# Places of TensorE's operands, dummy products ahead of runs of 256-column products, one more pair of feed-forward blocks by seven products, and half a conditioning vector made earlier

## The chip, the cores and the metric

The kernel runs on one core of a Trainium2 chip. The metric is the device time of one execution in microseconds (us), the median of the runs. TensorE is called PE in the profile, its weight loads PEld, VectorE DVE, ScalarE ACT, GpSimd POOL and SyncE SP.

## What is computed

Two layers over 512 tokens of width 1024, in float32. Layer 0 mixes tokens with a gated linear recurrence (hgrn2), layer 1 with attention in three dilated groups; each is followed by a gated feed-forward network (FFN) of inner width 2816.

```python
cond = silu(c)
h = x
for layer in range(2):
    mod = (cond @ ada_w[layer] + ada_b[layer])[:, None, :]
    sh1, sc1, g1, sh2, sc2, g2 = split(mod, 6)
    u = rms_norm(h, norm_g[layer, 0]) * (1 + sc1) + sh1
    y = hgrn2_mixer(u, ...) if layer == 0 else dilated_attention_mixer(u, ...)
    h = h + (1 + g1) * rms_norm(y, norm_g[layer, 1])
    u = rms_norm(h, norm_g[layer, 2]) * (1 + sc2) + sh2
    gate, up = split(u @ ffn_w_in[layer], 2)
    y = (silu(gate) * up) @ ffn_w_out[layer]
    h = h + (1 + g2) * rms_norm(y, norm_g[layer, 3])
```

The six vectors of `mod` are the conditioning vectors; the text writes (layer, number, half) for a half of 512, so (1, 1, 0) is the first half of layer 1's `sc1`.

## The kernel before

**Products of float32 values.** Every large operand is cut into two parts, a high part `hi` (rounded to the matmul's float32r type by ACT) and a low part `lo = x - hi` (DVE). One product of blocks is three matmuls: hi by hi, hi by lo, lo by hi. The activations stand in `uh` and `ul`, in the attention also, with the tokens in another order, in `apart` (two tiles). A matmul streams its moving operand, 512 or 256 columns, past a stationary operand (the weights that PEld loads, 128 columns). A row of the profile names them `out<-moving,stationary`. Products with 256 moving columns are called narrow here.

**FFN, first half.** `PLAIN = (3, 2)` says how many pairs of 256 columns of gate and up are made plainly in layer 0 and in layer 1: per pair 4 blocks of 24 matmuls with 512 columns (`block`, lines 577 to 579). The first pair is made in the stage before (`mixer_out`), by halves of the tokens. The other blocks of 128 columns, 22 - 2 * `PLAIN`, are made by `seven_products`: gate and up times the two halves of the tokens are a 2 by 2 product of blocks, done with seven block products instead of eight. Each of the seven is 12 narrow matmuls (`run`, line 964), so a block is 84. The sums of activations they need, `th` and `tl`, come from `token_sums` after the first plain pair; the sums of weights are made by POOL and DVE while PE works on the block before. The places of the cut weights (`ring`, `spare`) begin `R0 = 16` columns, 64 bytes, behind a multiple of 128 bytes; `uh`, `ul`, `th`, `tl` begin at multiples of 128 bytes. One of the seven products, `first`, uses the quarter B11 of the activations. For the first block it takes it where it stands; then `shift` copies this quarter 144 columns on (576 bytes, so 64 behind a multiple of 128), and every later block reads it there:

```python
B11 = [u_of(0, 0), [(uh[:, k, 144:400], ul[:, k, 144:400]) for k in range(4)]]
...
run(s.first, R, 0, B11[i > 0], True)
run(s.both, Sm, 1024, T3, True)
```

**Attention.** Queries and keys of two of the three groups are made by seven products as well (`sevens`, narrow, weights at `R0`, moving operands at multiples of 128 bytes), those of the third plainly with 512 columns. The values of two groups are made by `value_unit`, four times seven products of two by 12 narrow matmuls. There the activations are the stationary operand (multiples of 128 bytes) and the cut weights move; their places begin at `V0 = 32` columns, 128 bytes. All this is ordered by a planner (`Plan`): tasks with costs and due times are placed in a simulated run of the engines, and the order found is then issued as it is. `products` (line 1976) adds one task of 6 or 12 matmuls.

**Loads.** All weights come through one list, `items`, by SP's queue into a ring of two places `raw` of 1 MB; a load starts when the item two places earlier has been used. Items of the conditioning weights are woven between the others by `weave(list, others, first, every)`: one group of `others` after each `every` items of the list. Most conditioning halves are summed over k by DVE, four operations for each 1 MB item, and over the partitions by POOL (`partition_all_reduce`); for those in `sum_by_pe` the second sum is four PE products with `ones` (line 421), and for those in `by_pe` PE does both (line 372).

Of the kernel before, what the change touches and what calls it, by code (L numbers as in the profile page):

```python
# [11 lines left out]
F32 = mybir.dt.float32  # L12
# [5 lines left out]
P = 128  # L18
# [15 lines left out]
MAGIC = 12582912.0  # L34
WHOLE = ("quarters", "half")

R0, V0 = 16, 32


class Stream:  # L40
# [100 lines left out]
class Plan:  # L141
# [3 lines left out]
    DRAIN = {"DVE": 0.12, "ACT": 0.12}  # L145

    def __init__(self):
        self.tasks, self.names, self.seq = [], {}, {}

    def add(self, eng, cost, fn=None, r=(), w=(), goal=None, late=None, urgent=False):  # L150

# [85 lines left out]
    def run(self):  # L237

        ts = self.tasks
        for t in ts:  # L240
            for d in t["deps"]:
                ts[d]["outs"].append(t["id"])
        due = [0.0] * len(ts)
        for t in reversed(ts):
            at = min([due[o] - self.after(t, ts[o]) for o in t["outs"]], default=1e9)
            if t["goal"] is not None:
                at = min(at, t["goal"] + t["cost"])
            due[t["id"]] = at - t["cost"]
        tries = (self.trial(due, *rule) for rule in itertools.product((1, 2, 3, 5), (0.1, 0.2, 0.3), (5.0, 8.0, 1e9), (0.3, 1.0)))
        end, done, start = min(tries, key=lambda r: r[0])  # L250
        for t in done:
            t["start"], t["due"] = start[t["id"]], due[t["id"]]
        for t in done:
            if t["fn"]:
                t["fn"](t["eng"])
        return done
# [36 lines left out]
def block_kernel(tc, x, c, positions, ada_w, ada_b, norm_g, hgrn_w_in, lower, hgrn_norm_g, hgrn_w_out,  # L293
# [8 lines left out]
    with ExitStack() as ctx:  # L302
# [55 lines left out]
            return shared[:, 2 + turns_of_acc[0] % 2]  # L358

        by_pe = lambda l, v, hf: l == 0 and v in (2, 3, 4)  # L360
        sum_by_pe = lambda l, v, hf: by_pe(l, v, hf) or (l, v) == (1, 4)

        def ada_groups(l, v, hf, kq):

# [122 lines left out]
        items = []  # L487
# [6 lines left out]
        hg.append(win(W, 3 * D + 3 * 256))  # L494
        hg_o = [wtok(hgrn_w_out[0], kq, hf * 512) for hf in range(2) for kq in range(2)]

        PLAIN = (3, 2)

        def ffn_ws(l):

# [4 lines left out]
                a.append(("quarters", tuple(w[:, c:c + P].rearrange("(k p) n -> p k n", p=P) for c in (DFF + f * P, f * P))))  # L505
            return a, [wrow(ffn_w_out[l], j) for j in range(NF // 2)]

        items += weave(hg, ada_seq((0, 2), (0, 4), (0, 3), (1, 4)), 1, 0.7) + hg_o
        f0a, f0b = ffn_ws(0)
        n0 = 2 * PLAIN[0]  # L510
        gate, gate_fins = ada_halves(0, 5)
        one, two = ada_seq((1, 1)), ada_seq((1, 0))
        items += weave(f0a[:n0], [one[0], one[1], [], one[3][:1]], 2) + f0a[n0:]
        late = [gate[0], gate[1], gate[2], gate_fins[:1] + gate[3], one[2], gate_fins[1:] + one[3][1:], two[0], one[5] + two[1]]
        items += weave(f0b, late + two[2:], 0, 0.95)
        AW = attn_w_in[0]

        def av(g, hf):
# [363 lines left out]
        def seven_products(fs, mid, seeded, spare, th, tl):  # L882
# [5 lines left out]
            t_of = lambda i: [(th[:, i, k], tl[:, i, k]) for k in range(4)]  # L888
            B21, B22 = u_of(1, 0), u_of(1, 1)

            B11 = [u_of(0, 0), [(uh[:, k, 144:400], ul[:, k, 144:400]) for k in range(4)]]

            def shift():

                for a, b in ((112, 256), (0, 112)):
                    for copy, t in ((act.copy, uh), (dve.tensor_copy, ul)):
                        copy(t[:, 0:4, a + 144:b + 144], t[:, 0:4, a:b].bitcast(F32))
            t1, T3, T4, t2 = (t_of(i) for i in range(4))

            W = shared.rearrange("p a (b n) -> p (a b) n", b=2)  # L900
# [74 lines left out]
            with tc.manual_schedule(engines=ORDERED):  # L975
                r_hi(0)
                r_lo(0)
                sum_a(0)
                sum_b(0)
                sum_c(0)  # L980
                for k in range(2):
                    s_hi(0, k)
                    s_lo(0, k)
                r_hi(1)
                before = None
                for i in range(len(fs)):
                    more = i + 1 < len(fs)
                    R, Sm = places(i)
                    s = Sums(i)
                    run(s.first, R, 0, B11[i > 0], True)  # L990
                    run(s.both, Sm, 1024, T3, True)
                    if before:
                        gate_of(i - 1, before)
                    act.copy(s.u2, s.first)
                    if more:
                        r_lo(i + 1)
                        sum_a(i + 1)
                    if before:
                        value_of(i - 1, before)
                    run(s.u2, Sm, 0, t2, False)  # L1000
                    run(s.first, R, 1024, B21, False)
                    act.copy(W[:, 4 + i % 2], s.both)
                    act.copy(s.u4, s.u2)
                    if i == 0:
                        shift()
                    run(s.u4, Sm, 512, t1, False)
                    run(s.u2, R, 512, T4, False)
                    if more:
                        sum_b(i + 1)
                        s_hi(i + 1, 0)  # L1010
# [878 lines left out]
        def PE(cost, fn, r=(), w=()):  # L1889
            plan.add("PE", cost, lambda e: fn(), r, w, goal=clock[0])  # L1890
            clock[0] += cost
# [81 lines left out]
        def split_place(first):  # L1973
            return plan.place("hl", 3, lambda: st.part_tiles(first))

        def products(cost, dst, key, terms, begin, reads):


            def go():
                todo = [p for t in terms() for p in t]  # L1980
                for i, (x, y) in enumerate(todo):
                    pe.matmul(dst(), x, y, start=begin and i == 0, stop=i == len(todo) - 1, skip_group_check=True)  # L1982
            of_units.append(len(plan.tasks))
            PE(cost, go, reads, [key])

        triple = lambda xh, xl, yh, yl: ((xh, yh), (xh, yl), (xl, yh))
        a_of = lambda r, c: [[a[:, r * 4 + k, c * 256:c * 256 + 256] for a in apart] for k in range(4)]
# [117 lines left out]
        def plain(g, hd):  # L2105
# [16 lines left out]
            def both():  # L2122
# [4 lines left out]
                def one(i, t):  # L2127
                    b = mm_of()
                    for part in range(4):
                        def terms(part=part):  # L2130
                            for kt in (2 * part, 2 * part + 1):
                                w = slice((i * KT + kt) * P, (i * KT + kt + 1) * P)
                                yield triple(p.t[0][:, w], p.t[1][:, w], apart[0][:, kt], apart[1][:, kt])
                        products(6 * 0.2275, lambda: b.t, b(), terms, part == 0, [p("h", i), p("l", i)])
                    scale = SCALE if i == 0 else 1.0
                    for hf in range(2):
                        o = i * 64 + hf * 32
# [12 lines left out]
        def value_unit(i, hf):  # L2150
# [46 lines left out]
            def run(tag, tile, o, us):  # L2197
                b, p = mm_of(tag), ps[tile]
                for n in range(2):
                    def terms(n=n):  # L2200
                        for kt in range(4):
                            w = slice(o * 1024 + kt * 256, o * 1024 + (kt + 1) * 256)
                            yield triple(*us(kt, n), p.t[0][:, w], p.t[1][:, w])
                    products(12 * 0.1165, lambda n=n: b.t[:, n * 256:(n + 1) * 256], b(), terms, n == 0, [p("h", o), p("l", o)])
                return b

            def add_to(out, one, b, f):
# [293 lines left out]
```

## Time and profile before

| | |
|---|---|
| median of 3 runs | 1506.12 us (1504.59 to 1506.7) |
| profiled execution, its own time | 1504.35 us |
| its span | 1502.6 us |
| PE busy | 1476.8 us, 98% |
| PEld busy | 1323.5 us, 88% |
| DVE, ACT, POOL busy | 1095.8, 797.2, 191.3 us |
| bytes | 201.09 MB, mean 134 GB/s |

Matmuls overlap in the pipeline, so the length shown for one (276 to 281 ns for a narrow one) is not what it costs. What it costs is its pitch, the time from its start to the start of the next. A pitch is read here from a stretch that PE fills without a wait: its length over the number of matmuls that begin in it. In the view by windows the count of PE (x...) holds also the one or two that began just before the stretch.

The stages in the profiled execution: layer 0's mixer to about 300 us, the end of `mixer_out` to 341, layer 0's FFN to about 690, the attention to about 1110, layer 1's FFN after that, its narrow products from 1203.4 to 1376.5.

### The profile page before, as it was taken

Reading aid. Unit: us, or ns where it says so; the run is one execution under the profiler, and the core shown is the slowest. Engines: PE = TensorE matmul, PEld = TensorE weight load, DVE = VectorE, ACT = ScalarE, POOL = GpSimd, SP = SyncE. Lnnn points to the kernel's source line nnn. Section 1 sums busy time; section 2 is a strip of 40 time slices with the busy share of each in tenths; the row PEclk is TensorE's granted clock in tenths of the full one; section 3 lists DMA queues with packets and bytes.
Section 4 is the critical chain, followed back from the end, with each engine's and each line's share of the span. In section 5 each row is a group of like instructions: output and inputs, shape, how many; then the busy total and the mean of one; then the engine's idle time right before and its main releaser. Section 6 shows DMA issues by size and latency. Waiting matters only on the chain. (4 is left out here: it accounts for less than half of the span.)

```text
span 1502.6 us, 25061 instructions
## 1 busy us (share of the span) xinstructions
PE 1476.8 (98%) x9823; PEld 1323.5 (88%) x9823; DVE 1095.8 (73%) x1800; ACT 797.2 (53%) x1474; POOL 191.3 (13%) x172
## 2 busy tenths in 40 slices
PE   8999999999999999999999999999989999999998
PEld 6777788888999988788999999999978899999886
DVE  4587678487688885777798877888666978887533
ACT  4433343373455542267647878477875555555231
POOL 1011011031111100131001010001012211110100
PEclk9999999999999999999999999999999999999999
DMA  9654555124233346634344442345243333333531
GB/s 308 183 170 140 183 169 169 57 79 146 85 113 113 113 161 211 220 117 143 113 120 144 109 136 73 118 131 147 89 134 119 104 94 113 113 113 141 197 111 56
DMA packets 210151, 201.09 MB, mean 134 GB/s; under 512 B 8248, under 2 KB 167920, under 8 KB 209776
## 3 DMA queue, kind: packets, MB, share of 16 engines
q1 hardware_dynamic: 207056, 192.71, 41.3%
q10 hardware_dynamic: 1952, 6.65, 1.2%
q8 instruction: 77, 1.26, 0.4%
q0 software_dynamic: 1024, 0.13, 0.2%
q14 instruction: 42, 0.34, 0.1%
HBM read 192.31 MB, written 5.31 MB: 132 GB/s over the span
## 5 line engine op out<-in xcount | busy, mean ns | idle before, releaser
L90 ACT CAST hi<-raw 128x2048 fp32r<-128x2048 f32 x43 | 82.1, 1909 | 144.3 <-DMA raw<-in_ffn_w_out_dram 74.9
L91 DVE TENSOR_TENSOR lo<-raw,hi 128x2048 fp32r<-128x2048 f32 x43 | 103.7, 2413 | 65.7 <-ACT hi L90 65.6
L577 PE MATMUL ps_mm<-uh,hi 128*128 128x512 f32 (+1 forms) x400 | 145.6, 364 | 0.0
L578 PE MATMUL ps_mm<-ul,hi 128*128 128x512 f32 (+1 forms) x400 | 144.5, 361 | 1.1 <-DVE ul L677 1.1
L579 PE MATMUL ps_mm<-uh,lo 128*128 128x512 f32 (+1 forms) x400 | 143.9, 360 | 0.0
L1982 PE MATMUL ps_mm<-apart,hiq 128*128 128x256 f32 (+1 forms) x608 | 142.0, 326 | 0.1
L1982 PEld LDWEIGHTS ps_mm<-apart,hiq 128*128 128x128 f32 x608 | 100.0, 189 | 8.4 <-ACT xs L2096 0.3
L1982 PE MATMUL ps_mm<-apart,loq 128*128 128x256 f32 (+1 forms) x304 | 97.4, 321 | 0.4 <-DVE loq L2118 0.4
L964 PE MATMUL ps_mm<-tl,hiq 128*128 128x256 f32 x340 | 94.0, 276 | 0.0
L964 PE MATMUL ps_mm<-th,hiq 128*128 128x256 f32 x340 | 94.0, 276 | 0.0
L964 PE MATMUL ps_mm<-th,loq 128*128 128x256 f32 x340 | 94.0, 276 | 0.0
L955 DVE TENSOR_TENSOR loq<-raw,hiq 128x1024 fp32r<-128x1024 f32 x68 | 80.3, 1221 | 18.6 <-ACT hiq L951 18.6
L577 PEld LDWEIGHTS ps_mm<-uh,hi 128*128 128x128 f32 x400 | 75.2, 188 | 18.2 <-issue 6.7
L578 PEld LDWEIGHTS ps_mm<-ul,hi 128*128 128x128 f32 x400 | 75.4, 189 | 12.3 <-DVE ul L677 1.5
L579 PEld LDWEIGHTS ps_mm<-uh,lo 128*128 128x128 f32 x400 | 75.1, 188 | 12.4 <-issue 1.1
L578 PE MATMUL ps_mm<-lo,oh 128*128 128x512 f32 x208 | 81.5, 392 | 2.4 <-DVE lo L91 2.4
L935 POOL TENSOR_TENSOR raw<-raw 128x512 f32<-128x512 f32 x34 | 44.8, 1318 | 303.1 <-DVE spare L931 138.5
L577 PE MATMUL ps_mm<-hi,oh 128*128 128x512 f32 x208 | 81.5, 392 | 0.0
L951 ACT CAST hiq<-raw 128x1024 fp32r<-128x1024 f32 x68 | 68.0, 1047 | 18.7 <-DVE raw L939 17.1
L1982 PE MATMUL ps_mm<-uh,hiq 128*128 128x256 f32 x256 | 71.9, 281 | 0.0
L1982 PE MATMUL ps_mm<-uh,loq 128*128 128x256 f32 x256 | 71.3, 279 | 0.0
L1982 PE MATMUL ps_mm<-ul,hiq 128*128 128x256 f32 x256 | 71.3, 278 | 0.0
(479 smaller groups left out, 4632.8 us busy)
## 6 DMA issues: line engine op xcount, KB each, us to landing
raw<-in_ada_w_dram SPq DMA_DIRECT2D x40, 1024.0 KB, 5.1
raw<-in_ffn_w_in_dram SPq DMA_DIRECT2D x136, 256.0 KB, 4.1
raw<-in_ffn_w_out_dram SPq DMA_DIRECT2D x22, 1024.0 KB, 5.1
raw<-in_attn_w_in_dram SPq DMA_DIRECT2D x64, 256.0 KB, 4.6
raw<-in_hgrn_w_in_dram SPq DMA_DIRECT2D x12, 1024.0 KB, 5.3
raw<-in_attn_w_in_dram SPq DMA_DIRECT2D x12, 1024.0 KB, 5.2
raw<-in_ffn_w_in_dram SPq DMA_DIRECT2D x10, 1024.0 KB, 6.5
raw<-in_attn_w_in_dram SPq DMA_DIRECT2D x16, 512.0 KB, 4.6
```

What stands on the lines that cost most here:

```text
L90: self.nc.scalar.copy(hi, t)
L91: self.nc.vector.tensor_sub(lo, t, hi.bitcast(F32))
L577: pe.matmul(ps, ah, bh, start=start, stop=False, skip_group_check=part)
L578: pe.matmul(ps, ah, bl, start=False, stop=False, skip_group_check=part)
L579: pe.matmul(ps, al, bh, start=False, stop=stop, skip_group_check=part)
L935: pool.tensor_add(r[:, 2], r[:, 2], r[:, 0])
L951: act.copy(hi, src)
L955: dve.tensor_sub(lo, src, hi.bitcast(F32))
L964: pe.matmul(ps, w[x][:, a], us[kt][y], start=begin and kt + m == 0, stop=kt == 3 and m == 2, skip_group_check=True)
L1982: pe.matmul(dst(), x, y, start=begin and i == 0, stop=i == len(todo) - 1, skip_group_check=True)
```

## The change

```diff
-R0, V0 = 16, 32
+R0, V0 = 16, 48
...
+        narrow = []
+        for t in [t for t in done if t["eng"] == "PE"] + [{}]:
+            if t.get("narrow"):
+                narrow.append(t)
+                continue
+            first = next((k for k, u in enumerate(narrow) if u["aside"]), len(narrow))
+            if len(narrow) - first >= 12:
+                self.asides.add(narrow[first]["id"])
+            narrow = []
...
-        sum_by_pe = lambda l, v, hf: by_pe(l, v, hf) or (l, v) == (1, 4)
+        sum_by_pe = lambda l, v, hf: by_pe(l, v, hf) or (l, v) == (1, 4) or (l, v, hf) == (1, 1, 0)
...
-        PLAIN = (3, 2)
+        PLAIN = (2, 2)
...
-        items += weave(hg, ada_seq((0, 2), (0, 4), (0, 3), (1, 4)), 1, 0.7) + hg_o
+        one, two, own = ada_seq((1, 1)), ada_seq((1, 0)), ada_seq((0, 2), (0, 4), (0, 3), (1, 4))
+        items += weave(hg, own[:16] + [one[0], own[17] + one[1]], 1, 0.55) + hg_o[:1] + one[3][:1] + hg_o[1:]
...
-        n0 = 2 * PLAIN[0]
         gate, gate_fins = ada_halves(0, 5)
-        one, two = ada_seq((1, 1)), ada_seq((1, 0))
-        items += weave(f0a[:n0], [one[0], one[1], [], one[3][:1]], 2) + f0a[n0:]
         late = [...]
-        items += weave(f0b, late + two[2:], 0, 0.95)
+        items += f0a + weave(f0b, late + two[2:], 0, 0.95)
...
-            B11 = [u_of(0, 0), [(uh[:, k, 144:400], ul[:, k, 144:400]) for k in range(4)]]
-
-            def shift():
-
-                for a, b in ((112, 256), (0, 112)):
-                    for copy, t in ((act.copy, uh), (dve.tensor_copy, ul)):
-                        copy(t[:, 0:4, a + 144:b + 144], t[:, 0:4, a:b].bitcast(F32))
+            B11 = u_of(0, 0)
...
-                    run(s.first, R, 0, B11[i > 0], True)
+                    run(s.first, R, 0, B11, True)
+                    if i == 0:
+                        for _ in range(3):
+                            pe.matmul(s.both, R[0][:, 0:P], uh[:, 0, 16:272], start=True, stop=True, skip_group_check=True)
                     run(s.both, Sm, 1024, T3, True)
...
-                    if i == 0:
-                        shift()
...
+                for _ in range(3 if me in plan.asides else 0):
+                    pe.matmul(dst(), todo[0][0], aside(), start=True, stop=True, skip_group_check=True)
                 for i, (x, y) in enumerate(todo):
                     pe.matmul(dst(), x, y, start=begin and i == 0, stop=i == len(todo) - 1, skip_group_check=True)
...
-                    products(12 * 0.1165, lambda n=n: b.t[:, n * 256:(n + 1) * 256], b(), terms, n == 0, [p("h", o), p("l", o)])
+                    products(12 * 0.1165, lambda n=n: b.t[:, n * 256:(n + 1) * 256], b(), terms, n == 0, [p("h", o), p("l", o)],
+                             lambda: p.t[0][:, o * 1024 + 16:o * 1024 + 272])
```

In words. Layer 0's FFN makes one plain pair less and two blocks by seven products more. The shifted copy of B11 is gone. In its place stand three dummy products in each FFN, after the first block's first product; their results are written over by the product that follows. Their two operands both begin 64 bytes behind a multiple of 128, as those of the shifted product did. In `value_unit` the moving weights now begin 192 bytes behind, so 64 behind a multiple of 128, and the stationary activations still at multiples; three dummies with both operands at multiples of 128 go ahead of the first value product of each run of at least 12 narrow tasks. Two 1 MB loads for (1, 1, 0) move from layer 0's FFN into the mixer, whose conditioning items stand closer together (0.55 for 0.7), and PE makes the vector's second sum.

PE at the first block by seven products of layer 0's FFN; `ps_a` are sums, `uh`, `ul`, `th`, `tl` the activations and their sums, `spare` and `hiq`, `loq` cut weights. Before:

```order
L964 MATMUL ps_a_3368<-uh,spare_3081 128x256
L964 MATMUL ps_a_3368<-ul,spare_3081 128x256
L964 MATMUL ps_a_3368<-uh,spare_3082 128x256
L964 MATMUL ps_a_3370<-th_3084,hiq_3374 128x256
L964 MATMUL ps_a_3370<-tl_3085,hiq_3374 128x256
```

After:

```order
L965 MATMUL ps_a_3246<-uh,spare_3103 128x256
L965 MATMUL ps_a_3246<-ul,spare_3103 128x256
L965 MATMUL ps_a_3246<-uh,spare_3104 128x256
L994 MATMUL ps_a_3248<-uh,spare_3103 128x256 x3
L965 MATMUL ps_a_3248<-th_3106,hiq_3252 128x256
L965 MATMUL ps_a_3248<-tl_3107,hiq_3252 128x256
```

Three matmuls come between the first and the second product; layer 1's FFN has the same three.

PE at the first value products of the attention; `qk` are queries and keys, `apart` the stationary activations, `hiq` and `loq` the moving weights. Before:

```order
L1982 MATMUL ps_mm_6595<-apart_6292,loq_6471 128x256
L2248 MATMUL ps_a_6475<-qk_6472,qk_6468 128x128
L2248 MATMUL ps_a_6475<-qk_6472,qk_6468 128x256
L2248 MATMUL ps_a_6476<-qk_6472,qk_6468 128x256 x2
L1982 MATMUL ps_mm_6663<-hiq_6578,apart_6292 128x256
L1982 MATMUL ps_mm_6663<-loq_6579,apart_6292 128x256
```

After:

```order
L1986 MATMUL ps_mm_6686<-apart_6383,loq_6562 128x256
L2254 MATMUL ps_a_6566<-qk_6563,qk_6559 128x128
L2254 MATMUL ps_a_6566<-qk_6563,qk_6559 128x256
L2254 MATMUL ps_a_6567<-qk_6563,qk_6559 128x256 x2
L1984 MATMUL ps_mm_6754<-hiq_6669,apart_6383 128x256 x3
L1986 MATMUL ps_mm_6754<-hiq_6669,apart_6383 128x256
L1986 MATMUL ps_mm_6754<-loq_6670,apart_6383 128x256
```

Three dummies go ahead of these, and three more ahead of the third value product of the second run; the attention's order on PE is otherwise the same.

SP's loads in the mixer; `in_hgrn_w_in` are the mixer's weights, `in_ada_w` the conditioning weights. Before:

```order
L70 DMA raw_788<-in_ada_w_dram 128x4x512
L70 DMA raw_794<-in_hgrn_w_in_dram 128x8x256
L64 DMA raw_894<-in_ada_b_dram 128x512
L64 DMA raw_894<-in_norm_g_dram 128x512
L70 DMA raw_901<-in_ada_w_dram 128x4x512
L70 DMA raw_1027<-in_ada_w_dram 128x4x512
L70 DMA raw_1034<-in_hgrn_w_in_dram 128x8x256
```

After:

```order
L70 DMA raw_788<-in_ada_w_dram 128x4x512
L64 DMA raw_794<-in_ada_b_dram 128x512
L64 DMA raw_794<-in_norm_g_dram 128x512
L70 DMA raw_895<-in_ada_w_dram 128x4x512
L70 DMA raw_902<-in_hgrn_w_in_dram 128x8x256
L70 DMA raw_909<-in_ada_w_dram 128x4x512
L64 DMA raw_915<-in_ada_b_dram 128x512
```

Conditioning loads come earlier by up to one load of the mixer's weights, and the mixer's end holds two more.

More of the change, by code (lines that the diff above doesn't have):

```diff
@@ L147, in __init__ @@
     def __init__(self):
-        self.tasks, self.names, self.seq = [], {}, {}
+        self.tasks, self.names, self.seq, self.asides = [], {}, {}, set()
     def add(self, eng, cost, fn=None, r=(), w=(), goal=None, late=None, urgent=False):
@@ L1974, in split_place, with products @@
             return plan.place("hl", 3, lambda: st.part_tiles(first))
-        def products(cost, dst, key, terms, begin, reads):
+        def products(cost, dst, key, terms, begin, reads, aside=None, narrow=True):
+            me = len(plan.tasks)
             def go():
                 todo = [p for t in terms() for p in t]
+                for _ in range(3 if me in plan.asides else 0):
+                    pe.matmul(dst(), todo[0][0], aside(), start=True, stop=True, skip_group_check=True)
                 for i, (x, y) in enumerate(todo):
                     pe.matmul(dst(), x, y, start=begin and i == 0, stop=i == len(todo) - 1, skip_group_check=True)
-            of_units.append(len(plan.tasks))
+            of_units.append(me)
             PE(cost, go, reads, [key])
+            plan.tasks[me].update(narrow=narrow, aside=begin and aside is not None)
         triple = lambda xh, xl, yh, yl: ((xh, yh), (xh, yl), (xl, yh))
@@ L2133, in terms @@
                                 yield triple(p.t[0][:, w], p.t[1][:, w], apart[0][:, kt], apart[1][:, kt])
-                        products(6 * 0.2275, lambda: b.t, b(), terms, part == 0, [p("h", i), p("l", i)])
+                        products(6 * 0.2275, lambda: b.t, b(), terms, part == 0, [p("h", i), p("l", i)], narrow=False)
                     scale = SCALE if i == 0 else 1.0
```

## The prediction

> **What bounds the kernel now.** First the page's busy times:
>
> ```profile
> PE 1476.8 (98%) x9823; PEld 1323.5 (88%) x9823; DVE 1095.8 (73%) x1800; ACT 797.2 (53%) x1474; POOL 191.3 (13%) x172
> PEclk9999999999999999999999999999999999999999
> ```
>
> TensorE fills the span at a granted clock that no slice shows lowered. A matmul less, or a shorter pitch, is time gained at its full length, unless a wait swallows it. Second, PE's waits: the two up to 300 us (the mixer), and of the later ones the longest and the one that this change touches (columns: total us, times, longest).
>
> ```profile
> PE ps_a L1596 <- DVE aT L1589: 1.6, 1, 1.6
> PE ps_mm L372 <- DMA raw<-in_ada_w_dram: 0.6, 1, 0.6
> ...
> PE ps_a L2321 <- ACT h L2306: 2.7, 1, 2.7
> ...
> PE ps_mm L1982 <- DVE loq L2118: 0.4, 1, 0.4
> ```
>
> None lies among products by seven in the FFN, so a stage's end there moves with PE's work alone. Third, the chain of waits through the first blocks of layer 1's FFN, since pitch is what this change handles (start, length, matmuls):
>
> ```profile
> 1206.40 1.41 PE ps_mm L964 x12
> 1207.82 1.41 PE ps_a L964 x12
> 1209.23 4.24 PE ps_mm L964 x36
> 1213.47 2.81 PE ps_b L964 x24
> 1216.28 1.36 PE ps_mm L964 x12
> 1217.64 1.36 PE ps_b L964 x12
> 1219.00 4.08 PE ps_mm L964 x36
> ```
>
> The same narrow matmul costs 4.24/36 = 117.8 ns in the first block and 4.08/36 = 113.3 ns in the second. I call these the long and the short pitch. Between them stands 2.81: the shifted B11 run and the run behind it. By the code, in every other run one operand begins at a multiple of 128 bytes and the other 64 behind; in the shifted run both begin 64 behind. Taking that run at 118.4 each and the next at 115.8 (12 x 118.4 + 12 x 115.8 = 2810 ns), the places alike cost some 5 ns a product, and what follows them is short for a whole block. So both pitches occur with the same operands, and the short one has to be entered. Windows by block and stage say how much hangs on it:
>
> ```profile
> core 0: us, PE busy (x) PEld busy (x) DVE busy (x) ACT busy (x) POOL busy (x), PEclk, DMA share, GB/s
> 341.40:384.95 43.55, 43.55 (x195) 36.05 (x194) 30.80 (x37) 16.39 (x15) 5.82 (x3) 1.00 0.49 145
> 384.95:394.84 9.89, 9.89 (x85) 9.89 (x84) 5.27 (x6) 6.02 (x10) 0.00 (x0) 1.00 0.01 2
> 404.45:414.05 9.60, 9.60 (x86) 9.60 (x85) 7.82 (x8) 5.56 (x10) 1.29 (x1) 1.00 0.38 110
> 384.95:538.85 153.90, 153.90 (x1345) 153.90 (x1344) 119.84 (x128) 87.52 (x145) 18.22 (x15) 1.00 0.37 111
> 1203.40:1376.50 173.10, 173.10 (x1513) 173.06 (x1512) 135.97 (x143) 98.60 (x163) 20.66 (x16) 1.00 0.37 111
> ```
>
> They are: two plain pairs of layer 0 (192 matmuls of 512 columns), its first block by seven (long: 9.89/84 = 117.7 ns), a later block (9.60), and all 16 and 18 blocks of the two layers. 84 at the short pitch would be 9.52, so each shifted run costs 0.08 us. Granted clock is 1.00 in all of them, so the clock is not what separates the pitches.
>
> **The FFNs.** *The pair.* A plain pair of layer 0 is 43.55/2 = 21.78 us; it goes, and two blocks, 168 narrow matmuls, come. *The dummies.* With the shifted copies gone, B11 runs at opposite places, and the three dummies have the places that the shifted run had, left in the same way: the moving operand's place changes, the weights' doesn't. I expect them to do what it did, once, and the state to last through the stage, since PE waits nowhere in it. *The time.* Layer 0: first run 12 x 117.8 = 1.41, dummies 3 x 120 ns = 0.36, the other 1500 at 113.3 = 170.0, together 171.77 for 18 blocks, against 21.78 + 153.90 = 175.68 for the same work: 3.91 less. Layer 1: 171.77 for 173.10, 1.33 less. Cover for the two blocks more: DVE is busy 7.82 of 9.60 us in a block's window and the copies of `shift` are gone, so sums and casts keep up. Sum: 5.24.
>
> **The values.** Four windows of the attention: value run 1 (336 products, with 0.19 us of waiting at its entry), the products by seven behind it (60), value run 2 from its third product on (312), and a later stretch by seven (72).
>
> ```profile
> 733.35:773.85 40.50, 40.50 (x338) 40.47 (x337) 36.05 (x52) 19.00 (x27) 1.65 (x2) 1.00 0.34 108
> 777.58:784.64 7.06, 7.06 (x62) 7.06 (x61) 5.88 (x18) 3.48 (x8) 0.00 (x0) 1.00 0.86 226
> 940.97:978.00 37.03, 37.03 (x314) 37.03 (x313) 30.52 (x44) 15.37 (x24) 1.31 (x2) 1.00 0.43 127
> 809.93:818.09 8.16, 8.16 (x74) 8.16 (x73) 6.92 (x22) 5.89 (x17) 1.17 (x2) 1.00 0.59 153
> ```
>
> At V0 = 32 both operands begin at multiples of 128: (40.50 - 0.19)/336 = 120.0 ns, and 37.03/312 = 118.7. With 48 they are opposite. Two rows disagree on what that brings: 7.06/60 = 117.7 and 8.16/72 = 113.3, both opposite. The three dummies have places alike and are left by the moving operand's place, as in the FFN; value run 1 was left by the weights' place, and what followed was long. I take the short pitch: 336 x 113.3 + 0.36 + 0.19 = 38.62 for 40.50, 1.88 less; 312 x 113.3 + 0.36 = 35.71 for 37.03, 1.32 less. Sum 3.20; with the long pitch it would be 0.4 (39.58 + 0.55 = 40.13 and 36.75 + 0.36 = 37.11).
>
> A rule in the Trainium skill speaks against all of this: "TensorE: Matmul & The Clock Gate", Part 2, says that TensorE reads the streaming operand and the weights by two independent ports and that a weight load takes nothing from the running matmul; by it the places would be worth 0. The trace disagrees as far as it goes: 120.0, 117.7 and 113.3 ns for products alike in all but places and history.
>
> **What is late next.** PE comes to the stretch after value run 1 1.9 us sooner, and there it already waited 0.4 us for `loq` (L2118, DVE). DVE is busy 5.88 of 7.06 us there, so part of the gain turns into that wait: 0 to 1.9, I take 0.4, the size it has. The 2.7 us wait at L2321 stands at the end, where ACT waits for PE in turn: it moves along.
>
> **The mixer.** (1, 1, 0) leaves the FFN, where its loads cost PE nothing, and comes into the mixer:
>
> ```profile
> 60.00:300.00 240.00, 237.81 (x1408) 191.45 (x1407) 168.36 (x311) 90.70 (x182) 32.09 (x27) 1.00 0.46 150
> 148.72 0.95 PE L421 MATMUL ps_b<-ones,shared 128*128 128x1 f32 x8
> L394 DVE SCALAR_TENSOR_TENSOR shared<-raw,cond,shared 128x512 f32<-128x512 f32 x70 | 53.2, 760 | 14.2 <-DMA raw<-in_ada_w_dram 13.2
> raw<-in_ada_w_dram SPq DMA_DIRECT2D x40, 1024.0 KB, 5.1
> raw<-in_hgrn_w_in_dram SPq DMA_DIRECT2D x12, 1024.0 KB, 5.3
> 60.21 0.37 SPq L70 DMA_DIRECT2D raw<-in_hgrn_w_in_dram  x1
> ...
> 208.05 0.37 SPq L70 DMA_DIRECT2D raw<-in_hgrn_w_in_dram  x1
> ```
>
> Its second sum on PE is four `ones` products, as in the row: 0.95 us, all on the path (POOL's reduction goes; POOL bounded nothing). DVE's eight operations are 6.1 us, beside 72 us in which DVE is idle here. On SP's queue two 1 MB loads come ahead of the output weights, and all conditioning loads stand closer to the mixer's own: 1/0.55 = 1.8 MB of them for each weight item instead of 1/0.7 = 1.4, with POOL's and DVE's uses later by as little. Two loads cost 10.2 us if the queue were always full, nothing if never; its share is 0.46, and PE waited 0.6 us for a conditioning load in all. I take 0.2.
>
> **The sum**, on the profiled execution's own 1504.35 us: - 5.24 - 3.20 + 0.95 + 0.4 + 0.2 = - 6.9, so 1497.5; the median, 1506.12, stands 1.8 above it: 1499.2.
>
> **Rivals.** *R1, slower: the dummies don't bring the short pitch.* Then the shift, which did, is gone, and every block costs 9.89: 18 x 9.89 + 0.36 = 178.4 for 175.68 and for 173.10, + 8.0; the values save 0.4 without it; + 0.95 and + 0.2: 1506.12 + 8.8 = 1514.9. It decides at the pitch of the run after the dummies: 1.41 for 12, not 1.36. For it: three products instead of twelve, only one entry in a stage (today every block enters anew, so a lost state lasts one block), and a small stall in layer 1 that changed the pitch by itself:
>
> ```profile
> 1158.17 0.39 PE L578 MATMUL ps_mm<-ul,hi 128*128 128x256 f32 x1 [0.55 <-DVE ul L677]
> 1173.41:1181.57 8.16, 8.16 (x75) 8.16 (x73) 8.16 (x7) 5.78 (x5) 0.00 (x0) 1.00 0.46 131
> 318.89:321.60 2.71, 2.71 (x25) 2.71 (x24) 2.40 (x4) 1.23 (x3) 0.78 (x1) 1.00 0.03 6
> ```
>
> After that stall `mixer_out` runs at 8.16/72 = 113.3, while layer 0's runs at 2.71/23 = 117.8, one entering and one not. Against it: in all later blocks shifted runs entered, by places alone. 0.10.
>
> *R2: the FFN enters, the values don't* (as at 777.58): the values save 0.4 in place of 3.2, and PE's 0.4 wait doesn't grow: 1506.12 - 5.24 - 0.4 + 0.95 + 0.2 = 1501.6. For it the long 7.06; against it that the way of leaving differs. 0.15.
>
> *R3: the mixer's loads come late.* Three 1 MB loads per weight item (1 + 1.8) take 2.8 x 5.1 = 14.3 us if one follows the other, and the mixer's own weights are loaded every (208.05 - 60.21)/10 = 14.8 us (the quoted rows are the first and the last of eleven), so the ring would be at its limit: 10.2 x 0.46 = 4.7 us lost in place of 0.2, 1499.2 + 4.5 = 1503.7. For it: L394 already idles 13.2 us for these loads. Against it: PE waited 0.6 us for them, and two places let loads overlap. 0.12.
>
> *R4: places are without effect,* so the pitch stays what it is by other causes (the rule of the two ports would have it so): narrow products cost 153.90/1344 = 114.5 ns before and after. The pair saves 21.78 - 168 x 0.1145 = 2.5, twelve dummies cost 1.4, the mixer 1.15: 1506.1. 0.03.
>
> **How the numbers follow.** The forecast, 1499.2, has 0.58; its own range, 1495.7 (no `loq` wait, layer 0's `mixer_out` short as well, L1596's 1.6 us gone) to 1501. The rest, 0.02, is other mishaps. R2 and R3 bring it to 0.85, so the range is 1495.7 to 1504.0. What a measurement of this kernel can tell from no change is about 0.2%, 3 us. Faster by more: the forecast, R2 and a third of R3, 0.77; slower: R1 and 0.01 of mishaps, 0.11; within: 0.12.
>
> **What would show it.** In both FFNs the first run at 1.41, three matmuls at 0.12, then 1.36 for each 12 to the end of the stage, 171.8 from first to last; value runs of 38.6 and 35.7; a wait at L2118 no longer than 1 us; the mixer's end later by about 1 us, not 5. Wrong, if a run behind dummies takes 1.41, if a block midway falls back to 9.89, or if PE waits for `in_hgrn_w` or `in_ada_w` in the mixer.

## The result, and the profile after

| | before | after |
|---|---|---|
| median of 6 runs each | 1503.92 us (1502.73 to 1506.7) | 1496.26 us (1495.4 to 1500.53) |
| ratio, 95% interval | | 0.9953 [0.9941, 0.9965] |
| profiled execution, own time | 1504.35 us | 1495.76 us |
| its span | 1502.6 us | 1494.0 us |

The change makes the kernel faster by 0.47%, 5.3 to 8.9 us by the interval. The profile's answer to the rows of before starts with the windows of the changed kernel: the one plain pair that is left in the stage (with the first narrow product inside), the rest of the first run, the dummies with the run behind them, all that follows in layer 0 and in layer 1, and the two value runs.

```profile
342.45:364.41 21.96, 21.96 (x99) 18.14 (x98) 20.91 (x19) 8.46 (x9) 3.51 (x2) 1.00 0.33 94
364.41:365.71 1.30, 1.30 (x12) 1.29 (x11) 0.69 (x1) 0.00 (x0) 0.00 (x0) 1.00 0.14 43
365.71:367.44 1.73, 1.73 (x17) 1.73 (x16) 0.00 (x0) 0.36 (x1) 0.00 (x0) 1.00 0.00 0
367.44:536.08 168.64, 168.64 (x1490) 168.64 (x1489) 132.61 (x140) 96.30 (x160) 20.83 (x17) 1.00 0.39 113
1199.11:1367.75 168.64, 168.64 (x1490) 168.64 (x1489) 133.09 (x139) 96.30 (x160) 20.69 (x16) 1.00 0.38 113
730.83:769.47 38.64, 38.64 (x341) 38.61 (x340) 34.24 (x49) 18.33 (x26) 1.65 (x2) 1.00 0.36 113
938.11:973.86 35.75, 35.75 (x318) 35.75 (x316) 27.66 (x40) 15.37 (x24) 1.31 (x2) 1.00 0.43 121
```

Only one plain pair is left between `mixer_out` and the blocks (the first row). The first run's last 11 products take 1.30/11 = 118 ns; then come three dummies and twelve products in 1.73; then 1488 matmuls in 168.64 us, 113.3 ns each, in both layers without one lapse. The timeline of PE at the dummies (L994), start, length, matmuls:

```profile
365.59 0.28 PE L965 MATMUL ps_a<-uh,spare 128*128 128x256 f32 x1
365.71 0.52 PE L994 MATMUL ps_a<-uh,spare 128*128 128x256 f32 x3
366.06 0.29 PE L965 MATMUL ps_a<-th,hiq 128*128 128x256 f32 x1
366.18 0.28 PE L965 MATMUL ps_a<-tl,hiq 128*128 128x256 f32 x1
366.31 0.28 PE L965 MATMUL ps_a<-th,loq 128*128 128x256 f32 x1
366.42 0.28 PE L965 MATMUL ps_a<-th,hiq 128*128 128x256 f32 x1
```

From 366.06 on the starts are 0.12, 0.13, 0.11 apart, and 0.113 from there: the new pitch settles within four products. Next, two windows of the attention, before and then after: from the end of value run 1 to the third product of run 2, and a piece near the attention's end, from the last product ahead of a wait to the first one of the next line of work.

```profile
773.85:940.97 167.12, 166.28 (x1237) 157.22 (x1236) 136.66 (x325) 130.43 (x292) 15.87 (x16) 1.00 0.42 118
1114.67:1122.43 7.76, 4.83 (x16) 3.31 (x15) 2.94 (x17) 5.43 (x13) 0.00 (x0) 0.80 0.12 45
```

```profile
769.47:938.11 168.64, 166.93 (x1237) 157.16 (x1236) 138.01 (x328) 131.10 (x293) 16.20 (x16) 1.00 0.42 117
1110.55:1115.04 4.49, 3.36 (x17) 2.15 (x16) 1.82 (x13) 3.75 (x9) 0.00 (x0) 1.00 0.17 61
```

And the waits in them, of PE (in the first window, then in the second) and of DVE, before and then after:

```profile
PE ps_a L2273 <- ACT h L2329: 0.4, 1, 0.4
PE ps_mm L1982 <- DVE loq L2118: 0.4, 1, 0.4
...
PE ps_a L2321 <- ACT h L2306: 2.7, 1, 2.7
...
DVE wM L2298 <- DMA so<-scr: 4.6, 1, 4.6
```

```profile
PE ps_mm L1986 <- DVE loq L2123: 0.5, 1, 0.5
PE ps_a L2279 <- ACT h L2335: 0.4, 1, 0.4
PE ps_mm L1986 <- ACT xs L2101: 0.4, 1, 0.4
PE ps_mm L1986 <- ACT hiq L2122: 0.4, 1, 0.4
...
PE ps_a L2327 <- ACT h L2312: 0.9, 1, 0.9
...
DVE wM L2304 <- DMA so<-scr: 2.8, 1, 2.8
```

In the first windows the same 1235 or so matmuls take 1.52 us longer after, so most of the gain of value run 1 is given back. The second windows hold the same work, 7.76 us before and 4.49 after: DVE waits there for a small transfer (`so<-scr`), 4.6 us in the one execution and 2.8 in the other, PE waits behind it (2.7 and 0.9 us), and before, the granted clock fell to 0.80 over these 8 us. The fall is a piece of 3.4 us at half the clock, which begins 1.5 us after PE has work again. The same stands at this place in the traces of e1, e3, e5 and e11 below, and in no other trace. Here it is before, and in e5:

```profile
1119.30:1122.70 3.40, 3.40 (x12) 2.82 (x11) 0.37 (x1) 3.40 (x8) 0.00 (x0) 0.51 0.00 0
```

```profile
1120.50:1123.90 3.40, 3.40 (x13) 2.91 (x12) 0.96 (x1) 3.40 (x7) 0.00 (x0) 0.51 0.00 0
```

The page's row of PEclk doesn't show it: 3.4 us at half in a slice of 37.6 us leave 0.95, a 9.

The stages of all traces, as times between the starts of matmuls, in us: from the end of `mixer_out` to the end of the blocks by seven in layer 0 (F0) and layer 1 (F1), value run 1 (V1), from its end to the start of run 2 (gap), run 2 from its first product on (V2), and from its end to layer 1's `mixer_out` (tail). The last column is the ratio to the kernel before with its 95% interval.

| | F0 | V1 | gap | V2 | tail | F1 | ratio |
|---|---|---|---|---|---|---|---|
| before | 197.46 | 40.50 | 161.52 | 42.63 | 177.93 | 194.95 | 1 |
| after | 193.63 | 38.64 | 163.09 | 41.30 | 174.60 | 193.63 | 0.9953 [0.9941, 0.9965] |
| no FFN dummies (e1) | 199.93 | 38.64 | 163.84 | 41.30 | 177.24 | 199.93 | 1.0038 [1.0022, 1.0053] |
| one dummy (e2) | 200.05 | 38.41 | 162.88 | 41.06 | 174.47 | 200.05 | 1.0026 [1.0015, 1.0037] |
| values without dummies (e3) | 193.63 | 39.76 | 162.52 | 42.30 | 178.33 | 193.63 | 0.9958 [0.9941, 0.9974] |
| values as before (e4) | 193.63 | 40.50 | 161.73 | 42.63 | 174.80 | 193.63 | 0.9959 [0.9942, 0.9976] |
| left by the weights (e5) | 200.28 | 38.64 | 162.82 | 41.30 | 176.69 | 200.28 | 1.0030 [1.0013, 1.0047] |
| two dummies (e6) | 193.51 | 40.00 | 162.51 | 41.17 | 175.32 | 193.51 | 0.9949 [0.9934, 0.9964] |
| loads as before (e7) | 205.01 | 38.64 | 163.37 | 41.30 | 174.41 | 193.63 | 1.0030 [1.0013, 1.0048] |
| before, one pair less (e8) | 206.60 | 40.50 | 161.57 | 42.63 | 174.83 | 194.95 | 1.0070 [1.0053, 1.0086] |
| without pair and move (e9) | 196.31 | 38.64 | 164.18 | 41.30 | 174.28 | 193.63 | 0.9964 [0.9952, 0.9976] |
| sum by POOL, four (e10) | 193.75 | 40.24 | 161.49 | 41.41 | 174.95 | 193.75 | 0.9945 [0.9925, 0.9966] |
| fewest (e11) | 193.51 | 38.41 | 161.80 | 41.06 | 177.19 | 193.51 | 0.9930 [0.9912, 0.9948] |
| mixer at 0.7 (e12) | 193.63 | 38.64 | 163.24 | 41.30 | 174.63 | 193.63 | 0.9955 [0.9941, 0.9970] |

### The profile page after: what moved, and what is told of

The parts are those of the page before. It is cut to its first block, busy times and chain, and to the rows that moved or that the text cites. A ratio compares the mean times of both kernels' runs of the same rounds, so it can differ in the third digit from the quotient of the medians.

```text
span 1494.0 us, 25281 instructions
## 1 busy us (share of the span) xinstructions
PE 1468.6 (98%) x9915; PEld 1317.7 (88%) x9915; DVE 1100.7 (74%) x1800; ACT 799.1 (53%) x1484; POOL 193.1 (13%) x173
## 3 DMA queue, kind: packets, MB, share of 16 engines
q10 hardware_dynamic: 1952, 6.65, 1.2%
## 5 line engine op out<-in xcount | busy, mean ns | idle before, releaser
L91 DVE TENSOR_TENSOR lo<-raw,hi 128x2048 fp32r<-128x2048 f32 x41 | 98.9, 2414 | 59.8 <-ACT hi L90 59.6
L584 PE MATMUL ps_mm<-uh,hi 128*128 128x512 f32 (+1 forms) x368 | 133.2, 362 | 0.0
L585 PE MATMUL ps_mm<-ul,hi 128*128 128x512 f32 (+1 forms) x368 | 131.5, 357 | 1.1 <-DVE ul L684 1.1
L586 PE MATMUL ps_mm<-uh,lo 128*128 128x512 f32 (+1 forms) x368 | 131.4, 357 | 0.0
L965 PE MATMUL ps_mm<-th,hiq 128*128 128x256 f32 x360 | 99.4, 276 | 0.0
L965 PE MATMUL ps_mm<-tl,hiq 128*128 128x256 f32 x360 | 99.4, 276 | 0.0
L965 PE MATMUL ps_mm<-th,loq 128*128 128x256 f32 x360 | 99.4, 276 | 0.0
L584 PEld LDWEIGHTS ps_mm<-uh,hi 128*128 128x128 f32 x368 | 69.1, 188 | 15.7 <-issue 6.1
L585 PEld LDWEIGHTS ps_mm<-ul,hi 128*128 128x128 f32 x368 | 69.2, 188 | 12.8 <-issue 1.9
L586 PEld LDWEIGHTS ps_mm<-uh,lo 128*128 128x128 f32 x368 | 69.1, 188 | 10.1
```

Of the source, the lines that this page charges most:

```text
L91: self.nc.vector.tensor_sub(lo, t, hi.bitcast(F32))
L584: pe.matmul(ps, ah, bh, start=start, stop=False, skip_group_check=part)
L585: pe.matmul(ps, ah, bl, start=False, stop=False, skip_group_check=part)
L586: pe.matmul(ps, al, bh, start=False, stop=stop, skip_group_check=part)
L965: pe.matmul(ps, w[x][:, a], us[kt][y], start=begin and kt + m == 0, stop=kt == 3 and m == 2, skip_group_check=True)
```

## Experiments

Each is an edit of the changed kernel, but for e8, which edits the kernel before.

**e1: no dummies in the FFNs.**

```diff
-                        for _ in range(3):
+                        for _ in range(0):
```

> The changed kernel without the three dummies in the FFNs (those of the attention stay). Theory (the short pitch is a state that has to be entered, and the dummies enter it): both stages by seven run at 117.7 ns, 18 x 9.89 = 178.0 us for 171.7 each, so 12.6 us more than the changed kernel, about 5 us slower than the kernel before; attention as in the changed kernel. Rival (with one operand at a multiple of 128 bytes and the other 64 behind, a product is short by its places alone): 1504 x 113.3 ns = 171.3 us, the changed kernel less 0.7 us, 8 us faster than the kernel before.

Measured: 0.38% slower than the kernel before, 1510.08 us. A window over layer 0's blocks from the second run on:

```profile
365.71:543.68 177.97, 177.97 (x1513) 177.96 (x1512) 133.31 (x141) 98.37 (x161) 20.81 (x17) 1.00 0.37 108
```

1512 rows in 178.0 us are 117.7 ns each, and it stays so to the end, in both layers. The operands and their places are the same as in the changed kernel, where 113.3 stands. So the places alone don't set the pitch: it has to be entered, the dummies do that, and they are worth 6.3 us in each FFN (F0 and F1).

**e2: one dummy** at each place (`range(1)` in both loops).

> The changed kernel with one dummy in place of three, in both FFNs and at both places of the attention. Theory (any product with places alike, left by the moving operand's place, enters the short pitch): the same pitches at eight matmuls of 0.12 us less, so 1.0 us less than the changed kernel, 8.5 us faster than the kernel before. Rival (it takes several products to enter): FFN stages of 178.0 us in place of 171.7 and value runs at 117.7 ns, 12.6 + 2.9 us more, about 8 us slower than the kernel before.

Measured: half of each theory. The FFNs stay long, the value runs are short:

```profile
734.68:773.09 38.41, 38.41 (x340) 38.38 (x338) 34.42 (x50) 18.59 (x27) 1.65 (x2) 1.00 0.35 113
363.43:541.51 178.08, 178.08 (x1513) 178.07 (x1512) 133.40 (x141) 98.44 (x161) 20.91 (x17) 1.00 0.37 108
```

In the values one product with places alike is enough; in the FFN it is not. In the FFN that one dummy took 113 ns, and the products behind it 119, 119, 117, 119.

**e3: value weights at V0 = 48, no dummies there** (`range(0)` in `products`).

> The changed kernel without the dummies of the attention, value weights still 64 bytes behind a multiple of 128 (V0 = 48). Theory (state): the value runs follow products at the long pitch and stay there, 336 x 117.7 + 0.19 = 39.7 us and about 36.7 us in place of 38.6 and 35.7, some 2 us more than the changed kernel, 5.5 us faster than the kernel before. Rival (places alone): runs of 38.3 and 35.4 us, 0.7 us less than the changed kernel.

Measured: V1 39.76, V2 42.30, the long pitch as the theory of a state has it. The first twelve products of run 2 are an exception: behind a first step of 0.20 us the other eleven steps take 1.26 us (933.84 to 935.10), 114.5 ns each, with no dummy ahead of them. So a stall can enter the short pitch too, as the prediction read from its rows of `mixer_out`. The time, 0.9958, is not to be told from the changed kernel's: the gap behind V1 is 0.6 us shorter here and its tail, with the half clock, 3.7 longer.

**e4: values as before,** V0 = 32 and no dummies there.

> The changed kernel with the values as before: V0 = 32 (both operands at multiples of 128 bytes) and no dummies there. All theories of the FFN: its stages as in the changed kernel. Theory (places alike cost 120.0 and 118.7 ns): value runs of 40.5 and 37.0 us, 3.1 us more than the changed kernel, less what a wait of PE for the casts after the first run takes back in the changed kernel (1.0 us there by its profile): 2 to 3 us more, 4.5 to 5.5 us faster than the kernel before. Rival (the gain of the values is swallowed by waits): the same time as the changed kernel.

Measured: V1 40.50 and V2 42.63, as in the kernel before, so 3.2 us of PE time are back; but the gap is 161.73 in place of 163.09. From the start of V1 to the end of V2 it is 244.86 us here and 243.03 in the changed kernel: the values are worth 1.8 us by these two traces, and the ratios (0.9959, 0.9953) can't tell them apart. The expected 4.5 to 5.5 us faster was 6.2 by the ratio, within the interval.

**e5: dummies that are left by the weights' place.** Both operands at multiples of 128; the product that follows keeps the moving operand there and has its weights 64 behind.

```diff
-pe.matmul(s.both, R[0][:, 0:P], uh[:, 0, 16:272], start=True, ...
+pe.matmul(s.both, R[0][:, 16:16 + P], uh[:, 0, 0:256], start=True, ...
```

> The changed kernel with other operands in the FFNs' three dummies: both at multiples of 128 bytes (moving uh from column 0, weights 16 columns on), so that after them the weights' place changes and the moving operand's doesn't. Theory (the short pitch is entered when the moving operand leaves a place alike; value run 1 of the kernel before was left by the weights, and 117.7 ns followed): both FFN stages stay at 117.7 ns, 178 us each, as without dummies, 6 us slower than the kernel before. Rival (any products with places alike do it): 171.7 us each, 7 us faster than the kernel before.

Measured: both FFNs long, 1510.08 us. The window behind the dummies:

```profile
366.05:542.71 176.66, 176.66 (x1502) 176.66 (x1501) 132.59 (x140) 98.25 (x161) 20.76 (x17) 1.00 0.37 108
```

1500 in 176.66 is 117.8 ns. Three products with places alike are not enough by themselves. These three took 112, 117 and 119 ns by the starts of their rows, not 113, 120, 120 as the changed kernel's, so it stays open whether it is the leaving that fails, or already the coming into 120. The multiple of 128 by itself is not what fails: the dummies ahead of the value runs have both operands there too, are left by the moving operand, and V1 and V2 are short in this very run.

**e6: two dummies** everywhere.

> The changed kernel with two dummies in place of three everywhere. With one, the FFNs stayed long: that dummy took 113 ns and none took 120, while among three the second and third took 120. Theory A (one product at the 120 ns of places alike has to have gone by): two do it, pitches 113, 120, then the short pitch; FFN stages of 171.6 us, 0.5 us less than the changed kernel. Theory B (two are too few): FFN stages of 178 us, 12.6 us more. The attention enters in either case, as it did with one.

Measured: FFNs short, 193.51, as theory A has it (pitches 114, 119, then 121, 121, 116, 114). But value run 1 is long, and the last sentence expected was wrong:

```profile
730.66:770.66 40.00, 40.00 (x341) 39.97 (x340) 34.82 (x49) 18.87 (x27) 1.65 (x2) 1.00 0.34 109
```

One and three dummies entered there, two did not. At this place PE has a gap: from the first dummy's start to the next product's it is 305 or 306 ns in all these traces. Run 2, where this step is 121 ns, entered with two.

**e7: conditioning loads as before**, with the pair gone: `weave(hg, ..., 1, 0.7)`, the loads of (1, 1, 0) among layer 0's FFN weights, its second sum by POOL.

> The changed kernel with the conditioning loads as before: (1, 1, 0) in the FFN of layer 0 and its second sum by POOL, the mixer's items at 0.7. Theory (the move costs PE 0.95 us of sums and little else, and the FFN has cover for the two loads): the end of mixer_out 1 us earlier, at 341.4, layer 0's stage by seven unchanged at 171.7 us, in all 1 us less than the changed kernel, 8 us faster than the kernel before. Rival (without the plain pair the FFN of layer 0 has no room for these loads and DVE sums): PE waits there, by 2 to 6 us, for loads or cut weights.

Measured: the rival, and more than it asked: 0.30% slower than the kernel before. PE's waits in the first blocks, then SP's loads there, of this kernel and of the changed one:

```profile
PE ps_mm L967 <- ACT shared L1019: 7.3, 1, 7.3
PE ps_mm L967 <- ACT ps_mm L1000: 1.3, 1, 1.3
```

```profile
346.18 0.37 SPq L70 DMA_DIRECT2D raw<-in_ada_w_dram  x1
347.98 47.82 SPq L61 DMA_DIRECT2D raw<-in_ffn_w_in_dram  x20
```

```profile
335.42 59.01 SPq L61 DMA_DIRECT2D raw<-in_ffn_w_in_dram  x24
```

With a conditioning load ahead of them the weights of the first blocks begin to come at 348 instead of 335, their sums and casts run late, and the blocks, which have lost 21.8 us of lead with the plain pair, wait for them: F0 205.01 for 193.63, 11.4 us more. The waits are 8.6 of these; the window around them ran at a granted clock of 0.84, so part of the rest is slower products:

```profile
365.74:387.07 21.33, 12.71 (x89) 12.32 (x88) 11.65 (x21) 6.70 (x10) 5.77 (x3) 0.84 0.34 99
```

The late loads may not be all of it. In the same stretch DVE waits 3.5 us for POOL's second sum of (1, 1, 0) (`DVE diag L415 <- POOL shared L405`), which stands ahead of the next block's `loq` in its order, and this run doesn't tell the two apart. Either way, it is the move of (1, 1, 0) into the mixer that makes the pair's removal pay. Neither the density of the weave (e12) nor PE's second sum (e10) is needed for that.

**e8: the kernel before with PLAIN (2, 2) alone.**

> The kernel before with PLAIN (2, 2) alone: one plain pair less in layer 0, two blocks by seven more, shifted copy and V0 = 32 kept. Theory: 21.78 us go and 2 x 9.60 come, 2.6 us less, everything else as before. Rival (DVE or the loads in the shorter lead of layer 0's FFN are late): the gain is lost in waits there, 0 to 2 us slower than the kernel before.

Measured: the rival in kind, but 0.70%, 10.5 us, slower where it allowed 2: F0 206.60 for 197.46. The same two waits:

```profile
PE ps_mm L964 <- ACT shared L1015: 7.4, 1, 7.4
PE ps_mm L964 <- ACT ps_mm L994: 1.2, 1, 1.2
```

The kernel before didn't show them: its loads had 21.8 us more. As its loads, its copies and its values are those of the kernel before, the pair alone does this.

**e9: dummies and places without pair and move** (e7 with PLAIN (3, 2)).

> The changed kernel with PLAIN (3, 2) and the conditioning loads and POOL's sum as before: dummies and places alone, without the pair and without the move of (1, 1, 0). Theory (the parts add up): against the kernel before the FFNs save 16 x 0.08 - 0.36 = 0.9 and 17 x 0.08 + 0.3 - 0.36 = 1.3, layer 0's first block 0.3 more, the values 0.4 to 1.5 net, some 3 to 4 us in all; against the changed kernel 2.7 us for the pair less 1.0 for the mixer are missing, 1.7 more. Rival (pair and move carry the gain, dummies little): within 1 us of the kernel before.

Measured: 0.36% faster, 3.6 to 7.2 us. F0 falls by 1.15 and F1 by 1.32, as far as the sum expected (0.9 + 0.3, and 1.3); V1 and V2 by 3.2, of which the gap takes 2.7 back. The interval overlaps the changed kernel's, so the times don't show that pair and move together bring anything beyond this; by F0 it is 2.7 us, less what the mixer pays.

**e10: second sum of (1, 1, 0) by POOL, four dummies everywhere.**

```diff
-... or (l, v) == (1, 4) or (l, v, hf) == (1, 1, 0)
+... or (l, v) == (1, 4)
```

> The changed kernel with the second sum of (1, 1, 0) by POOL, its loads in the mixer as changed, and four dummies in place of three everywhere. Theory of the mixer (PE's four products are on its path): the end of mixer_out 0.95 us earlier; rival: the same, PE waits for something else there. Theory of the count (after the wait at the entry of value run 1 one and three dummies entered the short pitch and two did not, so an odd number is wanted there): value run 1 of 40.2 us at 117.8 ns, while run 2 (41.4) and both FFNs, where two and three entered, are short, 193.8 us from the end of mixer_out to the end of layer 0's blocks. Rival (two was an accident): value run 1 of 38.8.

Measured: F0 193.75, V2 41.41 and, with four, V1 long again:

```profile
729.02:769.25 40.23, 40.23 (x342) 40.20 (x341) 35.90 (x51) 18.97 (x27) 1.65 (x2) 1.00 0.34 109
```

So at value run 1 none (e3), one, two, three, four dummies gave long, short, long, short, long. An odd number fits that; two and four stand on one trace each, and why the gap brings it is not shown. The end of `mixer_out` came at 342.40 for 342.45, as the mixer's first plain product began 1.2 us later in this execution. From that product to `mixer_out` it is 239.3 here and 238.9 in e11, against 240.0 to 240.5 in the seven traces with the same loads and the sum on PE. That fits the theory that the 0.95 us is on the path and POOL hides it; the small waits of the mixer vary as well.

**e11: fewest.** Two dummies in each FFN, one at each place of the attention, the sum by POOL.

> The changed kernel with two dummies in each FFN, one at each place of the attention, and the second sum of (1, 1, 0) by POOL. Theory: everything enters the short pitch, 2 x 0.12 + 4 x 0.12 of dummies and 0.95 of sums less, 1.2 to 1.7 us less than the changed kernel, 8 to 9 us faster than the kernel before, if the sum by POOL hides; where it doesn't, as the changed kernel.

Measured: 1492.34 us, 0.9930 [0.9912, 0.9948]: the lowest ratio of all, 0.70% ahead of the kernel before, with an interval that overlaps the changed kernel's. Both FFNs and both value runs are short; the tail is long, with the half clock. Against the changed kernel the edits account for 0.24 us of dummies in the FFNs, 0.48 in the values and 1.1 to 1.6 in the mixer; the rest of the difference between the two ratios is within their intervals.

**e12: the mixer's items at 0.7,** the loads of (1, 1, 0) still there.

> The changed kernel with the mixer's conditioning items at 0.7 as before, but those of (1, 1, 0) still in the mixer, so that more of them stand at its end, ahead of the output weights. Theory (density costs nothing and is needed for nothing): the end of mixer_out at 342.5 us and layer 0's blocks as in the changed kernel. Rival (the closer weave is what makes room): the output weights or the first FFN weights come late, and PE waits 2 to 10 us there.

Measured: the same time, 0.9955, with a mixer 2 us longer (242.2) than in the seven traces above, so that `mixer_out` ends at 345.3, not at 342.5. But this execution has 3.4 us at half the clock in the mixer, which none of the seven has:

```profile
153.40:156.80 3.40, 3.40 (x34) 3.00 (x34) 0.85 (x2) 0.69 (x1) 0.00 (x0) 0.50 0.81 302
```

Half of 3.4 us, 1.7 by estimate, is most of the 2 us, so the trace shows no cost of the density that is clear of it. (e7 and e8 have the same piece, and a mixer of 240.9; the kernel before and e9, with the same loads and without it, have 239.3 and 239.2.) F0 is 193.63: the output weights and the blocks come in time. So the place of the two loads decides.

## Why the prediction was right, point by point

*Forecast and result.* 6.9 us less were forecast; the ratio says 7.1, 5.3 to 8.9. The median, 1496.26, is 2.9 under the forecast 1499.2 and just inside the range (from 1495.7): 2.2 of that is the kernel before itself, 1503.92 over six runs for the 1506.12 of three that the forecast starts from. The profile's 8.6 is more than the parts of the change explain.

*The FFNs* came out by their own steps. Layer 0 from the first product to the end: 0.12 + 1.30 + 1.73 + 168.64 = 171.79, forecast 171.77; layer 1 the same. F0 fell by 3.83 (3.91), F1 by 1.32 (1.33). R1, that the dummies don't do it, is out for three, and its price was sized rightly: e5, with three dummies and the long pitch, has 6.65 us more in each FFN, and 178.4 - 171.8 = 6.6 was forecast. Its first reason had something in it, since with one dummy R1 happens.

*The pair's cover* was the weak step. The prediction took DVE's share of a block's window as cover, and called the conditioning loads in layer 0's FFN free. They were free with three pairs. With two they would have cost 11.4 us of F0 (e7), and the move into the mixer, entered in the sum as a cost of 1.15 only, was the condition of the 3.91. The sum held because the change made both edits; that the move was a condition stood nowhere in it, and there it was lucky.

*The values:* V1 38.64 (38.62 forecast), run 2 35.75 (35.71). The waits behind run 1 were mis-sized: 0.4 was taken, with bounds of 0 to 1.9, and the gap grew by 1.6: `loq` hardly grew (0.5), but ACT's `xs` and `hiq` came to it with 0.4 each, and PE's busy time there grew by 0.65. Part of that is the same waits, since the end shown for a matmul is later than the start of the next: by the starts, 1.2 of the 1.6 arise at the three products that wait. In six traces with a V1 of 38.64 the gap is 162.8 to 164.2; in the three at 40.50, 161.5 to 161.7. So in these nearly all that V1 gains is swallowed (R2's outcome by another way), and 1.3 (V2) to 1.8 us (e4) stay of 3.2. It need not be: in e11, with a V1 of 38.41, there is no wait for `xs` or `hiq` and the gap is 161.80.

*The mixer:* its end is 1.05 us later, 1.15 forecast. By its stages it is 1.2 longer from its first plain product to `mixer_out` (240.5 for 239.3), began 0.3 later, and the last 120 products of `mixer_out` took 0.5 less: they ran at 113.3 ns, in the kernel before at 117.8. That half microsecond, which the range's lower end counted on, is luck: all the other traces have it, e8 with the mixer of the kernel before too. R3's late loads did not come, no wait of PE for `in_hgrn_w` or `in_ada_w` stands in the mixer from 60 us on. The 0.95 of PE's sum could be saved, as far as e10 and e11 show it.

*What hid the error:* the tail, 3.3 us shorter in the profile, which nobody forecast. It isn't the change: e8, with the attention of the kernel before, has 174.8, and the traces with the changed kernel's code there have 174.3 to 178.3. The prediction let the wait at L2321 move along with PE; it hangs on DVE's wait for `so<-scr`, which was 3.9, 4.6 and 4.1 us in the three longest tails (e3, before, e1) and 2.5 to 3.2 in the others. What divides long from short is the clock: the five tails of 176.7 and more (before, e1, e3, e5, e11) are the five with 3.4 us at half the clock behind this wait, and the nine others, 174.3 to 175.3, have none. So the profile's 8.6 is about 5 of the change and 3.3 of that. That the ratio's 7.1 stands so near the forecast's 6.9 is in part luck: how often each kernel meets the half clock there was not measured beyond one trace each.

*R4* is out: 1500 products with the same operands take 113.3 ns after three dummies and 117.7 without (e1), at a granted clock of 1.00 in both rows, and dummies with other places don't do it (e5). The rule of the two ports (the Trainium skill, "TensorE: Matmul & The Clock Gate", "Part 2: What happens when you issue a matmul": a weight load takes nothing from the running matmul) does not tell this case.

## What to carry to other kernels

Where a long run of narrow matmuls goes at a pitch above the best seen, look for what precedes it: two or three throw-away products, 0.24 to 0.36 us, bought 6.3 us in each FFN here, and their number has to be tried, not reasoned. An edit that shortens the lead of a stage is costed by what has to be loaded and prepared in that lead, not by how busy the engines are once the stage runs. And a gain ahead of a stage that waits for other engines may not arrive: read the stretch behind it before adding it to the sum. Last, a stage that the change doesn't touch can carry a good part of the difference of two profiles; the other traces with the same code in it tell whether it does.

## What the runs showed of the hardware that was not expected

- The pitch of this kernel's float32r matmuls of 256 columns is a state with a long memory: the same products kept 117.7 ns or 113.3 ns for 1500 matmuls, by what went by just before (e1). What in the engine holds the state is not shown.
- The number of products that enters the short state depends on the place: 2, 3 or 4 but not 1 in the FFN; 1 or 3 but not 0, 2 or 4 at value run 1, where the first step is 306 ns; any of 1 to 4 at run 2.
- A short wait of PE can cost more than its length. After the 2.7 us at L2321 the next six matmuls of 512 columns started 0.43 us apart (227 ns otherwise), with the granted clock at 0.80 over the window. Of the 14 traces, five have half the clock at this place, behind waits of 2.7, 2.3, 2.0, 1.2 and 1.0 us (before, e1, e3, e11, e5); nine have not, behind 0.6 to 1.3 us (1.3 in e4 and e6). So the length alone doesn't decide. In e11 the window has 0.59:

```profile
1108.84:1113.00 4.16, 4.16 (x19) 3.70 (x18) 1.63 (x2) 4.16 (x7) 0.00 (x0) 0.59 0.00 0
```
